# A two-layer mixture-of-experts backbone on one core: which experts share the 128 rows of a matmul unit, and the order in which their weights are loaded

## The chip, the cores and the metric

The kernel runs on one core of a Trainium2 chip. A core has a matrix engine (PE, TensorE), a vector engine (DVE), a scalar engine (ACT), a general engine (POOL, GpSimd) and a queue engine (SP) that issues most of the loads; 16 DMA engines move data between the chip's memory and the core's own buffers. The metric is the device time of one execution in microseconds (us).

## The reference

Two layers over 768 tokens (256 of context, 512 of a latent stream) of 1024 numbers each. Each layer is a mixer (projections, two attentions, a convolution, gates) and then a mixture of 32 experts. The change is in the second half, which the reference computes so:

```python
pg_top, g_sel = lax.top_k(pg, 1)                       # one of 4 groups of experts for a token
pe_top, e_sel = lax.top_k(jax.nn.softmax(le, axis=-1), TOP_K)   # two of the group's 8 experts
eid = g_sel * EXPERTS_PER_GROUP + e_sel
...
def expert_block(args):
    xe, e = args
    gu = xe @ w_gu[e]                                  # 1024 -> 512
    return (jax.nn.silu(gu[:, :D_EXPERT]) * gu[:, D_EXPERT:]) @ w_dn[e]   # 256 -> 1024
...
out = jnp.zeros_like(t).at[tok_buf].add(yb * w_buf[:, None])
```

Every token goes through two of the 32 experts, so that layer 0 has 1536 rows of work (768 tokens) and layer 1 has 1024 (only the 512 latent tokens are kept). All weights are 32-bit. An expert's weights are 3 MB, all 32 are 96 MB a layer, and every expert's weights are read once whatever the routing is.

## The kernel before

**Stages.** For each layer `mixer` runs the token mixers, `post` computes the mixer's output, the second norm and the routing, and `moe` runs the experts. In `moe` the rows of an expert's tokens are fetched by an indirect DMA (`gather`), turned by PE (`transposed`), multiplied (`up`, two halves, then `hidden` and `hidden_t`, then `down`) and written to the tokens' places in memory by another indirect DMA (`scatter`). A gather or scatter row with no token is skipped.

**Positions.** The program is fixed before the routing is known, so it is written for positions 0 to 31. Positions 0 to 4 are the five experts in `FIRST` (0, 8, 16, 24, 1), whose numbers are known beforehand. The other 27 experts stand in the order of their numbers of tokens, most first; `perm` holds that order, and `eid` the expert of each position.

**Units.** `moe` works in units of 128 rows. Before, `UNITS` says how many units hold one expert (128 rows of room), two (64 rows each) and four (32 rows each): 12, 6 and 2 in layer 0 and 8, 6 and 3 in layer 1, 20 and 17 units in all. Early positions are in the units of one. The five experts of `FIRST` come first, each alone in a unit; the others are spread evenly over the rest, and the last unit holds one expert. In a unit of two or four, `sides` cuts the 128 rows, and each matmul works on 64 or 32 rows with the weights of its expert.

**Loads.** An expert's weights come in three thirds of 1 MB: `up`'s first half, its second half, and `down`. `thirds` lists all 96 in the order in which the units use them: for each unit the first halves of its experts, their second halves, then the `down` thirds of the unit before. There are 16 slots (`slots_w`) of 1 MB in both layers. `load` puts third number k of the list in slot k mod 16, so that a load waits in SP's queue until the third 16 places ahead of it has been used; `consumed` asks for as many new loads as thirds have just been used. The first slots (`rx`) come free in `post`; the last four (`late`) exist only at its end. The first 14 thirds are of `FIRST` and are loaded before the routing is known; from the 15th on, SP must read `eid`.

**Order.** PE runs, for each unit: `up` of the first half, the turning of the unit before's hidden rows, the turning of the next unit's rows, `up` of the second half, `down` of the unit before. The rows of the last two units of a layer aren't scattered but are added by PE from `ends` at the end.

**Overflow.** If an expert has more tokens than its position has room for, `cni` is above zero and a slow general path runs (`tc.If(more > 0)`).

Of the kernel before, what the change touches and what calls it, by code (L numbers as in the profile page):

```python
# [8 lines left out]
F32 = mybir.dt.float32  # L9
# [5 lines left out]
ALU = mybir.AluOpType  # L15
AX = mybir.AxisListType
# [4 lines left out]
P = 128  # L21
# [5 lines left out]
NE = 32  # L27
# [5 lines left out]
FIRST = (0, 8, 16, 24, 1)  # L33

UNITS = ((12, 6, 2), (8, 6, 3))
RG = (3, 3)
RX = (4, 6)


@with_exitstack  # L40
def backbone(ctx: ExitStack, tc: tile.TileContext, x, c, ctx_in, c_ctx, w_ada, b_ada, w_in, sgu_gain, w_sgu,
# [1127 lines left out]
    def post(l, sl, sr, mixed, ms_done, res_src):  # L1169

        mh, ml, wA, y32, later = mixed
# [10 lines left out]
        slots_w = rx[3:] + rx[:3] + later + [lambda j=j: state["late"].tile([P, 2048], F32, name=f"late{j}_{l}")  # L1182
                                             for j in range(4)]
        state = {}


        n1, n2, n4 = UNITS[l]
        firsts = (0, n1, n1 + 2 * n2, NE)
        groups = [[tuple(range(p_, p_ + g)) for p_ in range(firsts[j], firsts[j + 1], g)] for j, g in enumerate((1, 2, 4))]

        units = groups[0][:len(FIRST)]
        last = groups[0].pop()
        del groups[0][:len(FIRST)]
        units += [u for _, _, u in sorted(((j + 0.5) / len(g_), len(g_[0]), u) for g_ in groups for j, u in enumerate(g_))]
        units.append(last)
        nu = len(units)

        def column(u):

            j = (1, 2, 4).index(len(u))  # L1200
            return sum(UNITS[l][:j]) + (u[0] - firsts[j]) // len(u)

# [6 lines left out]
        thirds += [(p_, 2) for p_ in units[-1]]  # L1209

        def load(p_, i, gu, dn):
# [54 lines left out]
        modulation("shift", 3)  # L1266
        rest = list(thirds)
        eid = pp.tile([1, NE], I32, name=f"eid{l}")
# [66 lines left out]
        def route(a):  # L1335
# [79 lines left out]
            T.matmul(pe[:, NE:2 * NE], ec[:, 1:2], perm, start=True, stop=True)  # L1415
            cn = rr.tile([1, 4], F32, name=f"cn{l}")
            for j in range(3):
                V.reduce_max(cn[:, j:j + 1], pe[:, NE + firsts[j]:NE + firsts[j + 1]], axis=AX.X)
                V.tensor_scalar(out=cn[:, j:j + 1], in0=cn[:, j:j + 1], scalar1=-float(P >> j), scalar2=0.0, op0=ALU.add,
                                op1=ALU.max)  # L1420
            V.reduce_sum(cn[:, 3:4], cn[:, 0:3], axis=AX.X)
            V.tensor_copy(cni, cn[:, 3:4])

        def placed(pt, ps):

            c0 = 0
            for j, g in enumerate((1, 2, 4)):
                w_ = P // g
                for h in range(g):
                    T.matmul(pt[w_ * h:w_ * h + w_, c0:c0 + UNITS[l][j]], ps[:, 0:w_], perm[:, firsts[j] + h:firsts[j + 1]:g],  # L1430
                             start=True, stop=True)
                c0 += UNITS[l][j]

# [158 lines left out]
        for i in sets:  # L1592
# [5 lines left out]
        return hs, w, st, (pp, tp, g1, raws, load, prefetch, rx, slots_w, yf, ms_done, rk, vv, vvs, ix, ig, cni, ws_, wv, lastp, units,  # L1598
                           column, placed, rank, firsts)

# [35 lines left out]
    def moe(l, sr, hs, st, nt, final=None):  # L1636
        (pp, tp, g1, raws, load, prefetch, rx, slots_w, yf, mixer_done, rk, vv, vvs, ix, ig, cni, ws_, wv, lastp, units, column,
         placed, rank, firsts) = st
        ntok = nt * P
# [105 lines left out]
        igo, iso = (pp.tile([P, 1], I32, name=f"{n_}{l}") for n_ in ("igo", "iso"))  # L1745
        wgo = pp.tile([P, 1], F32, name=f"wgo{l}")
        with tc.If(more > 0):
            cap = mp.tile([NE, P], F32, name="cap")
            cap2 = mp.tile([NE, P], F32, name="cap2")
            V.tensor_scalar(out=cap, in0=rank.to_broadcast([NE, P]), scalar1=firsts[1] - 0.5, scalar2=float(P // 2),  # L1750
                            op0=ALU.is_lt, op1=ALU.mult)
            V.tensor_scalar(out=cap2, in0=rank.to_broadcast([NE, P]), scalar1=firsts[2] - 0.5, scalar2=float(P // 4),
                            op0=ALU.is_lt, op1=ALU.mult)
            V.scalar_tensor_tensor(out=cap, in0=cap, scalar=float(P // 4), in1=cap2, op0=ALU.add, op1=ALU.add)
            pc = b("ax")[:, 0:NE]
# [7 lines left out]
            with tc.For_i(0, -(-(ntok - P // 4) // P), 1):  # L1763
                ino, ixo, wso = slots(mp, rko, vv, wv, nt, b)
                with tc.For_i(0, NE, 1) as e:
# [9 lines left out]
                    for i in range(2):  # L1775
                        up(pg, xT, (0,), i)
                    hT = hidden_t(hidden(pg))
                    py = b("y", D)
                    down(py, hT, (0,))
                    if l == 0:  # L1780
# [5 lines left out]
            for i in range(3):  # L1786
                load(0, i, w_gu[l, FIRST[0]], w_dn[l, FIRST[0]])

# [112 lines left out]
        for j, u in enumerate(units[-2:]):  # L1901
            scatter(None, col(ix, u) if l else ixe[:, j, 1:2], None)
        free = [s_ for s_ in range(len(slots_w)) if s_ >= RX[l]]
        yt, pts = {}, {}
# [220 lines left out]
```

## Time and profile before

| | |
|---|---|
| median of 3 runs | 1917.14 us (1915.33 to 1920.27) |
| the profiled execution's own time | 1918.57 us |
| its span, first to last instruction | 1916.8 us |
| mean granted TensorE clock, as a share of 2.4 GHz | 0.967 |
| PE busy | 1770.0 us (92%) |
| DVE, ACT and POOL busy | 1054.8, 616.1 and 218.1 us |
| read from and written to memory | 375.37 and 32.56 MB |
| mean rate over the span | 213 GB/s |

The shares are means over stages with different limits: the mixers do much arithmetic on few bytes, the experts the reverse. The experts of layer 0 run from about 786 to 1066 us, those of layer 1 from about 1629 us to the end.

### The profile page before, as it was taken

Reading aid. Unit: us, or ns where it says so; the run is one execution under the profiler, and the core shown is the slowest. Engines: PE = TensorE matmul, PEld = TensorE weight load, DVE = VectorE, ACT = ScalarE, POOL = GpSimd, SP = SyncE. Lnnn points to the kernel's source line nnn. Section 1 sums busy time; section 2 is a strip of 40 time slices with the busy share of each in tenths; the row PEclk is TensorE's granted clock in tenths of the full one; section 3 lists DMA queues with packets and bytes.
Section 4 is the critical chain, followed back from the end, with each engine's and each line's share of the span. In section 5 each row is a group of like instructions: output and inputs, shape, how many; then the busy total and the mean of one; then the engine's idle time right before and its main releaser. Section 6 shows DMA issues by size and latency. Waiting matters only on the chain. (4 is left out here: it accounts for less than half of the span.)

```text
span 1916.8 us, 25339 instructions
## 1 busy us (share of the span) xinstructions
PE 1770.0 (92%) x9530; PEld 1281.6 (67%) x9530; DVE 1054.8 (55%) x1921; ACT 616.1 (32%) x1212; POOL 218.1 (11%) x286
## 2 busy tenths in 40 slices
PE   5999999999999999699989699999999995998887
PEld 2888788888888898344433287788888895543322
DVE  3337888778778847444423456887344546221115
ACT  4425677222223323111100263676332432110001
POOL 2000121000000113211100100121000013111000
PEclk8999999999999999799999799999999997999989
DMA  8321003645567574799998824003323268699996
GB/s 299 88 85 53 1 2 98 203 162 171 164 205 249 191 267 192 277 320 402 419 417 337 224 79 128 9 1 127 110 83 110 67 236 314 236 373 421 420 421 194
DMA packets 144757, 390.80 MB, mean 204 GB/s; under 512 B 19844, under 2 KB 91892, under 8 KB 119028
## 3 DMA queue, kind: packets, MB, share of 16 engines
q1 hardware_dynamic: 128468, 356.48, 50.7%
q0 software_dynamic: 16160, 32.63, 5.5%
q8 instruction: 77, 1.26, 0.3%
q14 instruction: 52, 0.43, 0.1%
HBM read 375.37 MB, written 32.56 MB: 213 GB/s over the span
## 5 line engine op out<-in xcount | busy, mean ns | idle before, releaser
L58 PE MATMUL ps_pj<-hnh,wl 128*128 128x512 f32 (+1 forms) x1232 | 436.5, 356 | 15.6 <-ACT hnh L58 9.9
L58 PE MATMUL ps_pj<-hnl,wh 128*128 128x512 f32 (+1 forms) x1232 | 431.3, 350 | 0.9 <-DVE hnl L58 0.8
L58 PE MATMUL ps_pj<-hnh,wh 128*128 128x512 f32 (+1 forms) x1232 | 430.6, 350 | 0.0
L58 PEld LDWEIGHTS ps_pj<-hnh,wl 128*128 128x128 f32 x1232 | 233.3, 190 | 56.5 <-ACT hnh L58 14.2
L58 PEld LDWEIGHTS ps_pj<-hnl,wh 128*128 128x128 f32 x1232 | 233.9, 190 | 33.0 <-DVE hnl L58 1.9
L58 PEld LDWEIGHTS ps_pj<-hnh,wh 128*128 128x128 f32 x1232 | 233.9, 190 | 30.9 <-issue 0.2
L58 ACT ACTIVATE th<-ps_pj,vecT 128x256 f32<-128x256 f32 (+1 forms) x96 | 59.4, 619 | 353.9 <-PE ps_pj L58 311.0
L58 DVE SCALAR_TENSOR_TENSOR acc<-raw_ada,sT,acc 128x1024 f32<-128x1024 f32 x112 | 139.1, 1278 | 7.2 <-DMA raw_ada<-in_w_ada_dram 6.8
L58 PE MATMUL ps_gu<-rx,xT 128*64 128x512 f32 (+2 forms) x368 | 127.6, 643 | 7.5 <-DMA rx<-in_w_expert_gate_up_dram 7.4
L58 DVE COPY xT<-ps_tr 128x512 f32<-128x512 f32 x37 | 25.6, 691 | 162.0 <-PE ps_gu L58 99.6
L58 DVE SCALAR_TENSOR_TENSOR th<-th,ps_pb 128x256 f32<-128x256 f32 (+1 forms) x72 | 42.9, 596 | 124.7 <-PE ps_pb L58 88.7
L58 ACT ACTIVATE h<-ps_gu 128x256 f32<-128x256 f32 x37 | 14.2, 384 | 271.1 <-PE ps_gu L58 271.1
L58 DVE SCALAR_TENSOR_TENSOR yo<-ps_y,ws,g 128x1024 f32<-128x1024 f32 x33 | 42.3, 1283 | 101.4 <-PE ps_y L58 99.2
L58 PEld LDWEIGHTS ps_gu<-rx,xT 128*64 128x64 f32 (+2 forms) x368 | 40.0, 153 | 70.9 <-issue 55.2
L58 PE MATMUL ps_gu<-raw_m,xT 128*64 128x512 f32 (+2 forms) x176 | 81.2, 620 | 1.4 <-DMA raw_m<-in_w_expert_gate_up_dram 1.4
L58 PE MATMUL ps_gu<-late,xT 128*128 128x512 f32 (+2 forms) x192 | 76.1, 679 | 6.0 <-DMA late<-in_w_expert_gate_up_dram 6.0
L58 DVE TENSOR_TENSOR wl<-raw_g,wh 128x1024 fp32r<-128x1024 f32 x64 | 78.1, 1220 | 2.9 <-ACT wh L58 2.6
L58 DVE TENSOR_TENSOR pl<-ps_tr,ph 128x512 fp32r<-128x512 f32 x104 | 69.8, 686 | 13.0 <-ACT ph L58 12.0
L58 POOL DMA_INDIRECT y_d<-yo,ix x35 | 35.0, 1001 | 355.1 <-DVE yo L58 354.6
L58 PE MATMUL ps_gu<-raw_l,xT 128*128 128x512 f32 (+2 forms) x144 | 69.6, 625 | 5.4 <-DMA raw_l<-in_w_expert_gate_up_dram 5.4
L58 ACT ACTIVATE hT<-ps_h 128x256 f32<-128x256 f32 x37 | 14.2, 385 | 185.7 <-PE ps_h L58 185.7
L58 DVE TENSOR_REDUCE mx<-ps_sc 128x1 f32<-128x768 f32 (+1 forms) x80 | 67.0, 843 | 5.7 <-PE ps_sc L58 5.2
(481 smaller groups left out, 3564.4 us busy)
## 6 DMA issues: line engine op xcount, KB each, us to landing
raw_ada<-in_w_ada_dram SPq DMA_DIRECT2D x48, 1024.0 KB
rx<-in_w_expert_gate_up_dram SPq DMA_DIRECT2D x46, 1024.0 KB
raw_g<-in_w_gate_dram SPq DMA_DIRECT2D x32, 1024.0 KB
late<-in_w_expert_gate_up_dram SPq DMA_DIRECT2D x24, 1024.0 KB
late<-in_w_expert_down_dram SPq DMA_DIRECT2D x24, 1024.0 KB
raw_m<-in_w_expert_gate_up_dram SPq DMA_DIRECT2D x22, 1024.0 KB
raw_l<-in_w_expert_gate_up_dram SPq DMA_DIRECT2D x18, 1024.0 KB
raw_a<-in_w_expert_gate_up_dram SPq DMA_DIRECT2D x18, 1024.0 KB
```

Of the source, the lines that this page charges most:

```text
L58: ins = f(*a, **k)
```

## The change

The rows of a unit are cut in quarters of 32. `PLACES` gives each position a number of quarters, and `UNITS` lists, unit by unit, which sizes share it: "4" is one expert with 128 rows, "31" one with 96 and one with 32, "211" one with 64 and two with 32, "22" two with 64. Layer 0 has 18 units and layer 1 has 16. Positions 0 to 3, which hold four of `FIRST`, have 96 rows and share their units with experts of 32 rows; position 4 comes first, alone. In "31" and "211" units every matmul works on 32 rows, so an expert with 96 rows takes three matmuls for one block of weights.

The 15 thirds of `FIRST` are now all loaded before the others, and a later third takes the slot of the third whose use frees it (`place`). The order among the first 15 is by which slots are used up first over the stage. `placed` and the overflow count are rewritten for the new sizes, and the general path takes its rooms from `caps`.

```diff
-UNITS = ((12, 6, 2), (8, 6, 3))
+PLACES = ((4, 4, 12, 8), (3, 3, 9, 13))
+UNITS = ("4 31 31 31 31 22 4 22 31 22 31 4 22 31 22 31 22 4", "4 31 31 31 31 211 22 31 4 211 22 31 211 22 31 4")
...
-        units = groups[0][:len(FIRST)]
-        last = groups[0].pop()
-        del groups[0][:len(FIRST)]
-        units += [u for _, _, u in sorted(((j + 0.5) / len(g_), len(g_[0]), u) for g_ in groups for j, u in enumerate(g_))]
-        units.append(last)
+        quarters = _quarters(l)
+        of = {q: [p_ for p_ in range(NE) if quarters[p_] == q] for q in range(1, 5)}
+        kinds = [(k_, UNITS[l].split().count(k_)) for k_ in ("4", "31", "211", "22")]
+        tables = {}
+        for k_, n_ in kinds:
+            tables[k_] = []
+            for q in map(int, k_):
+                tables[k_].append((q, of[q][:n_]))
+                del of[q][:n_]
...
+            w_ = {"4": P, "22": P // 2}.get(k_, P // 4)
+            sl_, o_ = [], 0
+            for (q, _), p_ in zip(tables[k_], u):
+                sl_ += [(p_, slice(o_ + w_ * h, o_ + w_ * h + w_)) for h in range(32 * q // w_)]
+                o_ += 32 * q
+            parts_[u] = (sl_, k_)
...
+        loads_ = [x_ for x_ in thirds if x_[0] < len(FIRST)] + [x_ for x_ in thirds if x_[0] >= len(FIRST)]
+        place = {}
+        for k_, x_ in enumerate(loads_):
+            place[x_] = k_ if k_ < ns_ else place[thirds[k_ - ns_]]
+        ends_ = {place[x_]: n_ for n_, x_ in enumerate(thirds)}
+        n_first = 3 * len(FIRST)
+        early_ = sorted(range(n_first), key=lambda s_: ends_[s_])[:len(rx)]
+        turn_ = early_ + [s_ for s_ in range(ns_) if s_ not in early_]
+        slot_of = {x_: turn_.index(s_) for x_, s_ in place.items()}
+        loads_[:n_first] = [loads_[s_] for s_ in turn_[:n_first]]
...
-            s_ = thirds.index((p_, i)) % len(slots_w)
+            s_ = slot_of[p_, i]
...
-            cn = rr.tile([1, 4], F32, name=f"cn{l}")
-            for j in range(3):
-                V.reduce_max(cn[:, j:j + 1], pe[:, NE + firsts[j]:NE + firsts[j + 1]], axis=AX.X)
...
+            cn = rr.tile([1, NE + 1], F32, name=f"cn{l}")
+            V.tensor_tensor(out=cn[:, 0:NE], in0=pe[:, NE:2 * NE], in1=caps[l][0:1, :], op=ALU.subtract)
+            V.reduce_max(cn[:, NE:], cn[:, 0:NE], axis=AX.X)
+            V.tensor_scalar(out=cni, in0=cn[:, NE:], scalar1=0.0, scalar2=None, op0=ALU.max)
...
-            w_ = P // len(u)
-            return [(p_, slice(w_ * h, w_ * h + w_)) for h, p_ in enumerate(u)]
+            return parts_[u][0]
...
+def _quarters(l):
+    n = PLACES[l]
+    nf = len(FIRST) - 1
+    return [3] * nf + [4] * n[0] + [3] * n[1] + [2] * n[2] + [1] * n[3]
```

The rows below show how the instructions stand now. `ps_gu` is the result of `up`, `ps_y` of `down`; `rx`, `raw_l`, `raw_m`, `raw_a` and `late` are slots with a third of weights; `xT` and `hT` are turned rows.

PE in layer 1 before the change, the second unit (position 1 alone): its `up`, `down` of the first unit, and the third unit's `up`.

```order
L58 MATMUL ps_gu_14881<-rx5_1_13658,xT_14856 128x512 x4
L58 MATMUL ps_h_14887<-mats_60,h_14877 128x128 x2
L58 MATMUL ps_tr_14893<-mats_60,xg2_1_14598 128x128 x4
L58 MATMUL ps_tr_14899<-mats_60,xg2_1_14598 128x128 x4
L58 MATMUL ps_gu_14881<-rx0_1_13653,xT_14856 128x512 x4
L58 MATMUL ps_y_14927<-rx1_1_13654,hT_14890 128x512 x4
L58 MATMUL ps_gu_14948<-rx2_1_13655,xT_14892 128x512 x4
```

The same place after the change (positions 0 and 19):

```order
L62 MATMUL ps_gu_14995<-raw_l_14300,xT_14960 32x512 x3
L62 MATMUL ps_gu_14995<-late3_1_14649,xT_14960 32x512
...
L62 MATMUL ps_h_15014<-mats_60,h_14991 128x128 x2
L62 MATMUL ps_tr_15020<-mats_60,xg2_1_14700 128x128 x4
...
L62 MATMUL ps_gu_14995<-raw_a_14378,xT_14960 32x512 x3
L62 MATMUL ps_gu_14995<-rx3_1_13772,xT_14960 32x512
...
L62 MATMUL ps_y_15067<-rx5_1_13774,hT_15017 128x512 x4
```

The second unit now reads four thirds in its two `up` halves where it read two, and its second `up` half reads a third (in `rx3`) that is loaded only after the first unit has used that slot.

SP's queue at the end of `post` in layer 1 before the change, the last of the first 16 loads; `eid1` is the table that the routing writes.

```order
L1219 DMA late0_1_14521<-in_w_expert_gate_up_dram 128x2048
L1219 DMA late1_1_14523<-in_w_expert_down_dram 128x2048
L1279 TENSOR_LOAD eid1_13691
...
L1219 DMA late2_1_14535<-in_w_expert_gate_up_dram 128x2048
...
L1219 DMA late3_1_14547<-in_w_expert_gate_up_dram 128x2048
```

The same place after the change:

```order
L1255 DMA late0_1_14633<-in_w_expert_gate_up_dram 128x2048
L1255 DMA late1_1_14635<-in_w_expert_down_dram 128x2048
L1255 DMA late2_1_14637<-in_w_expert_down_dram 128x2048
L1315 TENSOR_LOAD eid1_13807
...
L1255 DMA late3_1_14649<-in_w_expert_gate_up_dram 128x2048
```

One load more (the 15th, in `late2`) stands ahead of the wait for the routing.

PE at the end of layer 1 before the change: `down` of the last unit but two (four experts), then `up` of the last unit, `down` of the last but one, and the last unit's second half.

```order
L58 MATMUL ps_y_16015<-raw_m_14388,hT_15987 32x512
L58 MATMUL ps_gu_16043<-raw_l_14390,xT_15989 128x512 x4
L58 MATMUL ps_y_16053<-late0_1_14521,hT_16051 64x512
L58 MATMUL ps_y_16053<-late1_1_14523,hT_16051 64x512
...
L58 MATMUL ps_gu_16043<-late2_1_14535,xT_15989 128x512 x2
```

After the change (the last unit but two holds two experts, the last but one 96 and 32 rows):

```order
L62 MATMUL ps_y_16301<-raw_m_14504,hT_16266 64x512
L62 MATMUL ps_gu_16321<-late3_1_14649,xT_16268 128x512 x4
L62 MATMUL ps_y_16331<-raw_l_14506,hT_16329 32x512 x3
L62 MATMUL ps_y_16331<-raw_a_14378,hT_16329 32x512
...
L62 MATMUL ps_gu_16321<-late0_1_14633,xT_16268 128x512 x2
```

The order of the steps is the same, and so is the number of thirds that the last unit and the one before it read in them.

## Rows read from the trace of the kernel before

**Rows 1.** The page: busy us by engine; GB/s moved in 40 slices

```profile
PE 1770.0 (92%) x9530; PEld 1281.6 (67%) x9530; DVE 1054.8 (55%) x1921; ACT 616.1 (32%) x1212; POOL 218.1 (11%) x286
...
GB/s 299 88 85 53 1 2 98 203 162 171 164 205 249 191 267 192 277 320 402 419 417 337 224 79 128 9 1 127 110 83 110 67 236 314 236 373 421 420 421 194
```

**Rows 2.** Stretches of both expert stages; last columns: clock, DMA share, GB/s

```profile
806.00:866.00 60.00, 60.00 (x192) 29.82 (x192) 26.45 (x31) 7.75 (x17) 10.12 (x10) 1.00 0.91 318
866.00:900.00 34.00, 34.00 (x148) 13.48 (x144) 15.06 (x18) 3.09 (x7) 5.07 (x5) 1.00 1.01 404
900.00:1030.00 130.00, 120.96 (x512) 46.78 (x508) 44.17 (x53) 12.62 (x29) 16.10 (x16) 0.97 1.02 419
...
1648.00:1704.00 56.00, 56.00 (x191) 26.50 (x193) 13.94 (x20) 6.77 (x15) 9.11 (x9) 1.00 0.90 319
1704.00:1752.00 48.00, 48.00 (x251) 18.52 (x243) 11.06 (x17) 5.42 (x12) 8.09 (x8) 1.00 1.02 419
1752.00:1840.00 88.00, 73.88 (x308) 24.76 (x308) 11.96 (x18) 5.95 (x14) 7.94 (x8) 0.94 1.02 421
1840.00:1862.00 22.00, 18.56 (x77) 5.25 (x78) 2.73 (x4) 1.24 (x3) 0.98 (x1) 0.84 1.01 419
...
1870.00:1874.00 4.00, 4.00 (x24) 0.96 (x17) 0.00 (x0) 0.00 (x0) 0.00 (x0) 0.57 0.74 309
...
1878.00:1882.00 4.00, 4.00 (x18) 1.06 (x16) 0.00 (x0) 0.00 (x0) 0.00 (x0) 1.00 0.27 105
```

**Rows 3.** The chain of work that ended last, layer 1: start us, us, what

```profile
1659.77 0.98 PE ps_tr L58 x8
...
1664.19 3.43 PE ps_y L58 x8
1667.62 3.43 PE ps_gu L58 x8
...
1671.28 0.96 PE ps_tr L58 x8
...
1702.83 3.57 PE ps_gu L58 x32
...
1714.96 3.63 PE ps_gu L58 x8
```

**Rows 4.** DMA queues from 1752 to 1840 us: packets, MB, share of 16 engines

```profile
q1 hardware_dynamic: 4763, 34.70, 94.6%
q0 software_dynamic: 1155, 2.33, 6.9%
```

**Rows 5.** SP's queue, layer 1: start us, us, issued loads, count

```profile
1636.34 8.63 SPq L1219 DMA_DIRECT2D rx<-in_w_expert_gate_up_dram  x2
1648.08 0.34 SPq L1219 DMA_DIRECT2D rx<-in_w_expert_down_dram  x1
...
1861.30 0.33 SPq L1219 DMA_DIRECT2D late<-in_w_expert_down_dram  x1
```

**Rows 6.** PE in order of time, ends of both stages; in brackets its waits

```profile
1036.61 3.65 PE L58 MATMUL ps_gu<-raw_a,xT 128*64 128x512 f32 x14 [1.33 <-DMA raw_a<-in_w_expert_gate_up_dram]
...
1051.66 3.70 PE L58 MATMUL ps_gu<-late,xT 128*128 128x512 f32 x8
...
1869.84 0.69 PE L58 MATMUL ps_y<-raw_m,hT 128*32 128x512 f32 x1 [1.42 <-DMA raw_m<-in_w_expert_down_dram]
...
1878.72 3.65 PE L58 MATMUL ps_y<-late,hT 128*64 128x512 f32 x16
1882.30 1.98 PE L58 MATMUL ps_gu<-late,xT 128*128 128x512 f32 x4
```

**Rows 7.** PE in order of time, the start of layer 1's experts

```profile
1628.78 1.95 PE L58 MATMUL ps_tr<-mats,y 128*128 128x128 f32 x8 [9.94 <-DMA y<-hn_d,ig]
```

**Rows 8.** Tile hn_d from 1560 to 1640 us: issue to landing

```profile
DMA to landing us min/median/max: 3.2/8.2/9.6
```

**Rows 9.** DVE in order of time, one row of the overflow count

```profile
1619.13 0.15 DVE L58 TENSOR_REDUCE cn<-ps_r 1x1 f32<-1x12 f32 x1
```

More of the change, by code (lines that the diff above doesn't have):

```diff
@@ L126, in backbone @@
     keyb, keyc, eidc = mats[0:NE, 656:688], mats[0:NE, 688:689], mats[0:NE, 689:690]
+    caps = [mats[0:NE, 700 + NE * l:700 + NE * l + NE] for l in range(2)]
     ones1 = cst.tile([P, P], F32, name="ones1")
@@ L1266, in post @@
         modulation("shift", 3)
-        rest = list(thirds)
+        rest = list(loads_)
         eid = pp.tile([1, NE], I32, name=f"eid{l}")
@@ L1415, in route @@
             T.matmul(pe[:, NE:2 * NE], ec[:, 1:2], perm, start=True, stop=True)
-            cn = rr.tile([1, 4], F32, name=f"cn{l}")
-            for j in range(3):
-                V.reduce_max(cn[:, j:j + 1], pe[:, NE + firsts[j]:NE + firsts[j + 1]], axis=AX.X)
[L1419 to L1422, printed above, removed]
-        def placed(pt, ps):
[L1426 to L1432, printed above, removed]
+            cn = rr.tile([1, NE + 1], F32, name=f"cn{l}")
+            V.tensor_tensor(out=cn[:, 0:NE], in0=pe[:, NE:2 * NE], in1=caps[l][0:1, :], op=ALU.subtract)
+            V.reduce_max(cn[:, NE:], cn[:, 0:NE], axis=AX.X)
+            V.tensor_scalar(out=cni, in0=cn[:, NE:], scalar1=0.0, scalar2=None, op0=ALU.max)
+        def placed(pt, ps):
+            for k_, n in kinds:
+                c0, o_ = first_col[k_], 0
+                for q, ps_ in tables[k_]:
+                    for p_ in ps_:
+                        if p_ == ps_[0] or p_ - 1 not in ps_:
+                            n_ = 1
+                            while p_ + n_ in ps_:
+                                n_ += 1
+                            cs = c0 + ps_.index(p_)
+                            T.matmul(pt[o_:o_ + 32 * q, cs:cs + n_], ps[:, 0:32 * q], perm[:, p_:p_ + n_], start=True,
+                                     stop=True)
+                    o_ += 32 * q
         def softmax_exp(src, mx, n, nm):
@@ L1598, in post @@
         return hs, w, st, (pp, tp, g1, raws, load, prefetch, rx, slots_w, yf, ms_done, rk, vv, vvs, ix, ig, cni, ws_, wv, lastp, units,
-                           column, placed, rank, firsts)
+                           column, placed, perm, parts_, free_)
     def spread(wv, vv, w, nt):
@@ L1746, in moe @@
         wgo = pp.tile([P, 1], F32, name=f"wgo{l}")
+        p0 = units[0][0]
         with tc.If(more > 0):
             cap = mp.tile([NE, P], F32, name="cap")
[L1749 to L1754, printed above, removed]
+            capp = mp.tile([NE, NE + 1], F32, name="capp")
+            V.tensor_tensor(out=capp[:, 0:NE], in0=perm, in1=caps[l], op=ALU.mult)
+            V.reduce_sum(capp[:, NE:], capp[:, 0:NE], axis=AX.X)
+            V.tensor_copy(cap, capp[:, NE:].to_broadcast([NE, P]))
             pc = b("ax")[:, 0:NE]
@@ L1775, in moe @@
                     for i in range(2):
-                        up(pg, xT, (0,), i)
+                        up(pg, xT, units[0], i)
                     hT = hidden_t(hidden(pg))
                     py = b("y", D)
-                    down(py, hT, (0,))
+                    down(py, hT, units[0])
                     if l == 0:
@@ L1786, in moe @@
             for i in range(3):
-                load(0, i, w_gu[l, FIRST[0]], w_dn[l, FIRST[0]])
+                load(p0, i, w_gu[l, FIRST[p0]], w_dn[l, FIRST[p0]])
         def place_weights():
@@ L1902, in moe @@
             scatter(None, col(ix, u) if l else ixe[:, j, 1:2], None)
-        free = [s_ for s_ in range(len(slots_w)) if s_ >= RX[l]]
+        free = list(free_)
         yt, pts = {}, {}
@@ L2073, in _constants @@
     m[:, 656:688], m[0:NE, 688], m[0:NE, 689] = key[None, :], key, np.arange(NE)
+    for l in range(2):
+        m[:, 700 + NE * l:700 + NE * l + NE] = 32 * np.array(_quarters(l))[None, :]
     def table(rot):
```

28 lines of the change are left out of this document (17 added, 11 removed).

## The prediction

> **What bounds the kernel now.** I read the page first: PE is busy 92% of the span and every other engine far less, but the rate of the DMA engines runs from 1 to over 420 GB/s [rows 1]. The two hills of 420 GB/s are the expert stages, and only there does the change act, so the next view is these stages cut into stretches [rows 2]. Each has two phases. At first (806 to 866 us in layer 0, 1648 to 1704 us in layer 1) PE is busy all the time at the full clock, 60.00 of 60.00 and 56.00 of 56.00 us, while the DMA engines move 318 and 319 GB/s. Later they move 419 to 421 GB/s, the highest steady rate, and PE has idle time: 73.88 of 88.00 us busy from 1752 to 1840 us. So a stage is bound by PE first and by the loads afterwards.
>
> The chain shows why. A unit with one expert takes PE from 1659.77 to 1671.28 us, 11.5 us; a unit with four takes from 1702.83 to 1714.96 us, 12.1 us [rows 3]. The price hardly depends on how many experts share a unit. The DMA price does. From 1752 to 1840 us the load queue brought 34.70 MB beside 2.33 MB of gathers and scatters [rows 4]; a third is 1.049 MB, so 33 thirds in 88 us, 2.66 us each with everything around them. One expert asks for 3 x 2.66 = 8.0 us of DMA per 11.5 us of PE: DMA idles. Four ask for 32 us per 12.1: PE idles. The five or more single units at the head of each layer waste DMA time that the quads miss later.
>
> That the low early rate is asked for and not suffered is seen in SP's queue: the 17th to 19th loads go out at 1636.34, some 8 us later, and 1648.08 us [rows 5], each when PE has used a third.
>
> **What the change does, part by part.** *Units.* After the first unit ("4"), four units of two experts each follow in both layers, then mostly pairs. Six thirds ask for 6 x 2.66 = 16.0 us of DMA per PE unit of about 12 (priced as the unit of four, the nearest row that works in 32-row pieces). Up to the third unit of layer 1 the slots come free as before, since the first unit still holds one expert: the third in hand at 1648 us is the same. From there two slots come free at almost every step of 3.4 us (`up` or `down`, [rows 3]) and two thirds cost 5.3 us, so the queue in front of the DMA engines grows, and the rate should be 420 GB/s from the third unit on.
>
> What that is worth is the bytes not moved early, at the full rate. Layer 1: (421 - 319) x 56 / 421 = 13.6 us. Layer 0: (421 - 318) x 60 / 421 = 14.7 us, and (421 - 404) x 34 / 421 = 1.4 us [rows 2]. Together 29.7 us, the most that this can give, since the same 96 thirds and the same token rows are still moved.
>
> Three things are taken off or left open.
> - *The ramp.* With one or two loads outstanding the engines will not reach 421 at once. If one unit of 12 us still runs at the old rate, that is 12 x 102/421 = 2.9 us a layer. Bounds are nothing and two units, 0 to 11.6 us in all; I take 5.8, since the queue grows by about 4 us of work a unit.
> - *Uneven engines.* At the end the rate falls from 309 (1870 us) to 105 GB/s (1878 us) [rows 2]: some of the 16 engines finish about 8 us ahead of the last. The last, which decides, is some 3.5% slower over the 234 us from 1648, so it had less idle time early: 3.5% of 56 or 60 us, 2 us a layer. Bounds 0 and 8 us in all; I take 4.
> - *The last steps.* Before, PE's last wait for a load ends at 1869.84 us for the 91st third, and the last unit's second half starts at 1882.30 us, 12.5 us later, which is five thirds at 2.49 us (1.049 MB at 421 GB/s). In layer 0 it is 1036.61 and 1051.66 us, 15 us for six [rows 6]. So the end of the loads and the last `up` coincide. After the change the last `down` but one needs the 94th third, two places before the end, and takes 3.6 us (the `ps_y` row at 1878.72 us [rows 6]): the last `up` then starts 5.0 - 3.6 = 1.4 us before the last third lands. At half clock (0.57 at 1870 us [rows 2]) it takes near 7 and starts 2 us after. I take 0, with 2 us either way per layer.
>
> *Loads.* The 15th third no longer waits for the routing. 1 MB more, 2.5 us, stands in front of the normed rows `hn_d`, whose write takes up to 9.6 us to land [rows 8], and on which the first gather of layer 1 waits (PE idle 9.94 us [rows 7]). But the same megabyte is then missing beside that gather. I take 0, with 2.5 us either way a layer. The second unit's second `up` half needs a third loaded only after 1636.34 us; it is used after the third load's issue at 1648.08 us, over 10 us later [rows 5], and the longest landing seen, 9.6 us, fits. If it came late, PE would wait there, but the end hangs on the loads, which no longer wait for PE.
>
> *Small parts.* Matmuls on 32 rows: 12.1 against 11.5 us a unit, some 0.6 us in each of four early units, on PE, which has 4 us to spare per unit as soon as the loads bind; without that cover, 5 us in both layers. `placed` goes from 7 matmuls to 6 in layer 0 and to 8 in layer 1. The overflow count goes from eight short DVE steps (0.15 us [rows 9]) to three, while PE waits for the first gather [rows 7]: nothing. The overflow path stays shut: with the reference's inputs the fullest position by this table has 30 tokens in 32 rows in layer 0 and 27 in 32 in layer 1. Gathers, scatters and their bytes are unchanged; two and one units fewer save PE some 12 us each, while PE waits for loads: nothing.
>
> **The sum.** 29.7 - 5.8 - 4 = 19.9 us. The profiled execution took 1918.57 us with 1.8 us around its span: 1898.7 us. It was 1.4 us above the median of the runs shown, so against the median 1917.14 - 19.9 = 1897 us.
>
> **Rivals.**
> *The engines were nearly full already.* The share column says 0.90 and 0.91 in the early stretches against 1.02 later [rows 2]. If that is the room there is, it is (1.02 - 0.90) x 56 / 1.02 + (1.02 - 0.91) x 60 / 1.02 + 0.3 = 13.4 us, with half the ramp and the 4 us off about 6.5: 1910.5 us. For it: the column. Against it: the same engines move 421 at 1.02, so at 0.90 they should move 371, and they move 319; a packet that waits alone counts as busy. The Trainium skill has a rule that points the same way (DMA: Bandwidth & Descriptors, "Where 436 GB/s comes from"): loads from memory are bound at about 358 GB/s per core. By that page alone the room would be (358 - 319) x 56 / 358 + (358 - 318) x 60 / 358, an estimate of 12.8 us; this trace, with 421 GB/s of loads for 88 us, differs, and the sum goes by the trace.
>
> *No net change.* The start slips by 2.5 us in each layer, the ramp takes two units, the last engine gains least, and the last steps run at half clock: 29.7 - 11.6 - 8 - 5 - 4 = 1 us, 1916 us. Each is possible, all at once hardly.
>
> *Slower: PE's clock.* Where the loads bind, PE works 12 us in 16, 75%, and in pieces. The granted clock was 0.94 with PE busy 84% from 1752 us, 0.84 from 1840 us, and 0.57 for 4 us after waits near 1870 us [rows 2]. If the mean clock falls below 12/16 = 0.75, PE becomes the bound again: at 0.65 a unit takes 18.5 us, 2.5 us above its loads, and over some nine such units in each layer that is 45 us: 1897 + 45 = 1942 us. Against it: a slower PE waits less, and the clock came back to 1.00 after each dip in these rows. The Trainium skill (TensorE: Matmul & The Clock Gate, "HAM oscillation") tells of a kernel that lost its clock at every wait for a load; here the row at 1870 us agrees with a dip, and the row from 1752 us, at 0.94, with no lasting one.
>
> **How the numbers follow.** The forecast, a gain of 10 to 30 us (1887 to 1907), has a chance of 0.75. The nearly full engines have 0.13, no change 0.05, the clock 0.07. The low end is the most that the bytes can give with the last steps as well, 1917 - 29.7 - 2 = 1886; the high end takes in most of the second case, 1910. About 0.3%, 5.8 us (1911.4), is what a measurement here tells from no change. Faster has the forecast's 0.75 and, of the nearly full engines, 0.08; same 0.05 + 0.05; slower 0.07.
>
> **What would show it.** Right: in each layer the rate passes 400 GB/s about two units after the stage's start instead of five to seven; in layer 1 PE begins to wait for loads some 40 us earlier after the stage's start than before, where it was still busy 48.00 of 48.00 us up to 1752 us [rows 2]; layer 1's stage begins 10 to 13 us earlier, and its last `up` some 20 us earlier than 1882.30 us. Wrong: an early rate that stays near 340 with a share of 1.0 (the first rival), a clock below 0.75 over the second half of a stage (the last), or a first gather that lands 2 us later. A PE that waits in the second to fifth unit would show that the shared units starve, which costs nothing unless the DMA engines idle meanwhile.

## The result, and the profile after

The changed kernel takes 1891.81 us (median of 4 runs, 1889.62 to 1893.32), the kernel before 1917.79 us in the same comparison: a ratio of 0.9866 (0.9849 to 0.9883), 26 us less. A second comparison, on another chip, gave 0.9865 (0.9845 to 0.9885). The forecast was 1897 us; the gain is 6 us larger than the 20 us foreseen.

The page of the kernel after, the lines that answer to [rows 1]: busy us by engine and the rate in 40 slices.

```profile
span 1891.5 us, 26769 instructions
...
PE 1739.8 (92%) x10296; PEld 1256.8 (66%) x10296; DVE 1042.1 (55%) x1895; ACT 611.2 (32%) x1203; POOL 210.5 (11%) x280
...
GB/s 304 90 76 64 1 2 72 209 171 170 170 196 209 265 249 171 273 367 419 418 417 355 226 79 126 15 1 129 88 107 84 94 186 340 254 419 421 418 418 196
```

PE's share is the same 92%, and it tells nothing here: the hills of 420 GB/s begin earlier in each expert stage, and this is seen only when a stage is cut up. Stretches of the kernel before that were not shown yet, from the turning of the first gathered rows to the second half of the last `up`, whole and at both ends (us, busy us and instructions of PE, PEld, DVE, ACT and POOL, granted clock, DMA share, GB/s):

```profile
786.10:806.00 19.90, 19.90 (x77) 10.55 (x78) 5.12 (x16) 1.99 (x5) 5.43 (x6) 0.86 0.59 207
786.10:1051.66 265.56, 254.16 (x988) 107.45 (x988) 99.06 (x124) 26.22 (x60) 38.67 (x39) 0.98 0.93 368
1030.00:1051.66 21.66, 19.30 (x69) 6.83 (x66) 8.25 (x8) 0.77 (x2) 1.95 (x2) 1.00 0.69 286
1628.78:1648.00 19.22, 19.22 (x72) 10.23 (x73) 3.74 (x10) 1.99 (x5) 4.01 (x4) 0.84 0.35 131
1860.00:1882.30 22.30, 18.93 (x70) 5.16 (x66) 2.13 (x3) 0.77 (x2) 0.98 (x1) 0.92 0.72 297
1628.78:1882.30 253.52, 232.59 (x950) 89.80 (x950) 45.56 (x70) 22.14 (x51) 31.11 (x31) 0.95 0.91 365
```

The same stretches of the kernel after:

```profile
789.13:815.00 25.87, 25.87 (x142) 12.57 (x142) 5.81 (x17) 2.96 (x7) 4.04 (x4) 0.89 0.56 188
815.00:870.00 55.00, 55.00 (x412) 20.19 (x409) 24.96 (x29) 5.80 (x13) 8.10 (x8) 1.00 1.01 414
...
1020.00:1039.31 19.31, 16.70 (x76) 5.12 (x72) 4.55 (x5) 0.77 (x2) 1.75 (x2) 1.00 0.69 282
789.13:1039.31 250.18, 233.78 (x1350) 88.00 (x1350) 88.15 (x112) 23.27 (x54) 32.16 (x32) 0.99 0.94 383
1615.61:1640.00 24.39, 24.39 (x140) 12.10 (x140) 4.44 (x11) 2.96 (x7) 6.83 (x7) 0.89 0.51 175
1640.00:1690.00 50.00, 50.00 (x424) 18.30 (x424) 12.13 (x18) 5.80 (x13) 8.10 (x8) 1.00 1.01 416
1690.00:1840.00 150.00, 127.62 (x712) 42.27 (x704) 23.88 (x34) 10.94 (x26) 15.02 (x15) 0.94 1.01 419
1840.00:1857.06 17.06, 16.05 (x84) 5.58 (x84) 2.13 (x3) 0.77 (x2) 0.97 (x1) 1.00 0.64 265
1615.61:1857.06 241.45, 218.06 (x1352) 78.24 (x1352) 42.58 (x66) 20.46 (x48) 30.92 (x31) 0.95 0.94 383
```

Read them as engine time lost against 421 GB/s. In layer 1, before, the first 19.22 us lost 19.22 x (421 - 131)/421 = 13.2 us and the next 56 us, at 319 GB/s [rows 2], 13.6 us; after, the first 24.39 us lose 14.3 and the next 50 us 0.6. That is 26.8 against 14.9: 11.9 us, and the stage is 12.1 us shorter. The ends, at 297 and 265 GB/s, lost 6.6 and 6.3. In layer 0 the stage is 15.4 us shorter, but it also moves less, 95.86 MB against 97.61 before, and the 1.75 MB loaded ahead of it are worth 4.2 us at 421 GB/s. Where PE waits for loads in layer 1 the clock was 0.94 (1690 to 1840 us); before it was 0.94 and then 0.84 [rows 2].

SP's queue after, layer 1 (start, us, issued loads, count), against [rows 5]:

```profile
1622.91 0.36 SPq L1255 DMA_DIRECT2D rx<-in_w_expert_gate_up_dram  x1
1631.89 0.33 SPq L1255 DMA_DIRECT2D raw_m<-in_w_expert_gate_up_dram  x1
1635.48 0.33 SPq L1255 DMA_DIRECT2D raw_l<-in_w_expert_gate_up_dram  x1
1636.06 0.33 SPq L1255 DMA_DIRECT2D late<-in_w_expert_down_dram  x1
1640.46 0.33 SPq L1255 DMA_DIRECT2D raw_a<-in_w_expert_gate_up_dram  x1
1641.05 0.33 SPq L1255 DMA_DIRECT2D rx<-in_w_expert_gate_up_dram  x1
```

From 1635 us on, 20 us into the stage, two slots come free at almost every step. The chain of work that ended last (start, us, what), against [rows 3]:

```profile
1660.87 3.57 PE ps_gu L62 x32
1664.44 3.48 PE ps_y L62 x32
1667.92 16.77 DMA rx<-in_w_expert_gate_up_dram
1684.81 24.92 DMA raw_l<-in_w_expert_gate_up_dram
1709.84 23.82 DMA rx<-in_w_expert_down_dram
```

Where the chain of before went through PE from unit to unit, it now passes to the loads at 1667.92 us, 52 us into the stage. PE in order of time, layer 1 (in brackets its waits), against [rows 6, 7]:

```profile
1615.61 1.95 PE L62 MATMUL ps_tr<-mats,y 128*128 128x128 f32 x8 [6.96 <-DMA hn_d<-hn]
...
1709.77 0.62 PE L62 MATMUL ps_gu<-raw_l,xT 128*32 128x512 f32 x1 [1.25 <-DMA raw_l<-in_w_expert_gate_up_dram]
...
1846.13 0.64 PE L62 MATMUL ps_y<-raw_m,hT 128*64 128x512 f32 x1 [0.42 <-DMA raw_m<-in_w_expert_down_dram]
...
1857.06 1.98 PE L62 MATMUL ps_gu<-late,xT 128*128 128x512 f32 x4
```

Before, the first wait for a load in this stage was:

```profile
1757.97 0.62 PE L58 MATMUL ps_gu<-rx,xT 128*32 128x512 f32 x1 [0.90 <-DMA rx<-in_w_expert_gate_up_dram]
```

So PE first waits for a load 94 us into the stage, where it was 129 us before. Not all went well: layer 0's first gathered rows are turned at 789.13 us, 3.0 us later than before, though the order of the experts, `perm`, was known at nearly the same time.

### The profile page after: what moved, and what is told of

Read it like the earlier page. It is cut to its first block, busy times and chain, and to the rows that moved or that the text cites. A ratio compares the mean times of both kernels' runs of the same rounds, so it can differ in the third digit from the quotient of the medians.

```text
span 1891.5 us, 26769 instructions
## 1 busy us (share of the span) xinstructions
PE 1739.8 (92%) x10296; PEld 1256.8 (66%) x10296; DVE 1042.1 (55%) x1895; ACT 611.2 (32%) x1203; POOL 210.5 (11%) x280
## 5 line engine op out<-in xcount | busy, mean ns | idle before, releaser
L62 PE MATMUL ps_gu<-late,xT 128*32 128x512 f32 (+2 forms) x296 | 109.4, 622 | 9.5 <-DMA late<-in_w_expert_gate_up_dram 9.5
L62 PE MATMUL ps_gu<-rx,xT 128*32 128x512 f32 (+2 forms) x448 | 101.5, 618 | 8.0 <-DMA rx<-in_w_expert_gate_up_dram 8.0
L62 PE MATMUL ps_gu<-raw_m,xT 128*32 128x512 f32 (+2 forms) x272 | 95.7, 635 | 9.1 <-DMA raw_m<-in_w_expert_gate_up_dram 9.0
L62 DVE SCALAR_TENSOR_TENSOR yo<-ps_y,ws,g 128x1024 f32<-128x1024 f32 x30 | 38.5, 1284 | 106.6 <-PE ps_y L62 106.6
L62 PE MATMUL ps_gu<-raw_l,xT 128*32 128x512 f32 (+2 forms) x328 | 90.6, 613 | 1.3 <-DMA raw_l<-in_w_expert_gate_up_dram 1.3
L62 DVE TENSOR_TENSOR pl<-ps_tr,ph 128x512 fp32r<-128x512 f32 x104 | 69.8, 687 | 12.9 <-ACT ph L62 11.9
L62 ACT ACTIVATE pr<-ps_sc,mx 128x768 f32<-128x768 f32 (+1 forms) x80 | 65.8, 824 | 13.2 <-DVE mx L62 12.4
L62 ACT CAST wh<-raw_g 128x1024 fp32r<-128x1024 f32 x64 | 66.7, 1042 | 6.6 <-DMA raw_g<-in_w_gate_dram 6.6
L62 PE MATMUL ps_pb<-ycl,bh 128*128 128x256 f32 (+1 forms) x192 | 68.3, 356 | 0.0
```

The costliest lines, as they stand in the source:

```text
L62: ins = f(*a, **k)
```

## The experiments

Each kernel was compared with the kernel before on the same chip. The table beside the medians is from one profiled execution each: the time from `perm` to the first turning of gathered rows in layer 0 (start 0) and layer 1 (start 1), and from there to the last `up` (stage 0 to its second half, stage 1 to the second block of it), all in us.

| kernel | median | ratio to before (95%) | start 0 | stage 0 | start 1 | stage 1 |
|---|---|---|---|---|---|---|
| before | 1917.79 | 1 | 7.71 | 265.56 | 12.93 | 257.25 |
| after | 1891.81 | 0.9866 (0.9849 to 0.9883) | 10.46 | 250.18 | 11.02 | 245.17 |
| after, again | 1894.26 | 0.9865 (0.9845 to 0.9885) | 12.13 | 250.24 | 10.80 | 244.80 |
| old shares, new code | 1923.66 | 1.0026 (1.0016 to 1.0035) | 11.53 | 264.26 | 11.11 | 257.29 |
| the same, 15th load late | 1920.81 | 1.0015 (1.0002 to 1.0029) | 8.02 | 265.03 | 11.20 | 256.83 |
| new shares in layer 1 only | 1914.13 | 0.9964 (0.9950 to 0.9977) | 12.53 | 265.03 | 11.16 | 245.10 |
| first five alone | 1917.59 | 0.9987 (0.9976 to 0.9997) | 12.42 | 261.49 | 11.28 | 254.53 |
| one unit more a layer | 1901.49 | 0.9907 (0.9892 to 0.9922) | 10.83 | 252.48 | 12.11 | 249.64 |
| 15th load late | 1888.00 | 0.9842 (0.9825 to 0.9859) | 8.57 | 249.90 | 10.89 | 244.54 |
| 13th to 15th late | 1895.06 | 0.9870 (0.9848 to 0.9893) | 8.59 | 252.73 | 12.36 | 244.14 |
| first pair | 1888.85 | 0.9838 (0.9816 to 0.9859) | 11.18 | 246.98 | 12.55 | 240.70 |
| first pair, 15th late | 1887.33 | 0.9830 (0.9813 to 0.9847) | 7.89 | 247.60 | 13.06 | 241.32 |
| first pair, 13th to 15th late | 1893.63 | 0.9874 (0.9857 to 0.9891) | 7.86 | 251.01 | 13.48 | 242.03 |

The time of one kernel moves by some 5 us either way between executions (the kernel before: 1914.09 to 1924.92 in 21 runs). Much of that lies outside the stages: from the last `up` of layer 0 to layer 1's `perm` the profiled executions take 558.8 to 566.0 us, while the two of the changed kernel agree within 0.4 us in both stages. So a step of the kernel is read from the columns and the sum from the ratios. Start 0 is not so steady: 10.46 and 12.13 us in these two.

**Old shares, new code.** In this and the following kernels `HEADS` gives the quarters of the first five positions, `PLACES` counts the other 27, and "1111" is a unit of four.

```diff
+HEADS = ((4, 4, 4, 4, 4), (4, 4, 4, 4, 4))
-PLACES = ((4, 4, 12, 8), (3, 3, 9, 13))
+PLACES = ((7, 0, 12, 8), (3, 0, 12, 12))
-UNITS = ("4 31 31 31 31 22 4 22 31 22 31 4 22 31 22 31 22 4", "4 31 31 31 31 211 22 31 4 211 22 31 211 22 31 4")
+UNITS = ("4 4 4 4 4 4 22 4 22 1111 4 22 4 22 4 22 1111 4 22 4", "4 4 4 4 4 22 1111 4 22 22 1111 22 4 22 1111 22 4")
```

> The new code with the old shares: the first five positions with 128 rows each and the 20 and 17 units of before, so that only the new order of the first 15 loads and the rewritten small parts are left of the change. Theory (the gain is bytes that the early shared units pull forward): nothing of the gain is left, 1917 us, within 3 of the kernel before, and the early rate in layer 1 is back near 319 GB/s. Rival 1 (the gain comes from the 15th load ahead of the routing and the new order of the slots): 1892 to 1905 us.

Measured: 1.0026, 5 us slower than before. The whole gain is gone and a cost appears; rival 1 falls. Both stages are as long as before, within 1.3 us. Its early stretches, to be compared with 318 and 319 GB/s in [rows 2]:

```profile
811.00:871.00 60.00, 60.00 (x192) 29.42 (x193) 26.91 (x31) 7.52 (x17) 11.15 (x11) 1.00 0.91 315
...
1651.00:1707.00 56.00, 56.00 (x194) 26.43 (x196) 14.06 (x20) 6.78 (x15) 9.11 (x9) 1.00 0.90 321
```

So the shares alone are worth 1.0026 - 0.9866 = 0.016 of the time, some 31 us, and the code around them costs some 5 us.

**New shares in layer 1 only.** The first halves of `HEADS`, `PLACES` and `UNITS` as in the last kernel, the second halves as in the changed one.

> The old shares in layer 0, the new ones in layer 1. Theory: layer 1 keeps what its own rows say, 12 us of its stage and some 2 us at its start, so 1904 us (1900 to 1907), and layer 0's stage is as before. Rival 2 (the gain is in the number of units, 20 to 18 and 17 to 16, at some 8.7 us for each of the three): layer 1 keeps one third, 1909 us.

Measured: 0.9964, 1914 us, above what either expected. As a ratio the rival's 1909 us is 0.9954, inside the interval (0.9950 to 0.9977), so the time alone doesn't exclude it. Against the old shares in the same code it is 0.0062, 12 us, and the rows place them: stage 1 is 245.10 us, as in the changed kernel, stage 0 265.03 us, as before. The expectation had left out the 5 us that the new code costs. In the profiled execution the first `ps_po` of layer 0, ahead of anything edited, also came 3.8 us later than with the old shares (679.7 against 675.9 us). Rival 2's one third of the gain doesn't fit the rows: layer 1 loses one unit of the three, and its stage gets 12 of the 26 us by which both stages are shorter than with the old shares.

**First five alone.** The new sizes, but the sharing of the first five positions taken away; their small partners share one unit.

```diff
+HEADS = ((4, 4, 4, 4, 4), (4, 4, 4, 4, 4))
-PLACES = ((4, 4, 12, 8), (3, 3, 9, 13))
+PLACES = ((3, 4, 12, 8), (2, 3, 9, 13))
-UNITS = ("4 31 31 31 31 22 4 22 31 22 31 4 22 31 22 31 22 4", "4 31 31 31 31 211 22 31 4 211 22 31 211 22 31 4")
+UNITS = ("4 4 4 4 4 22 4 22 31 22 31 1111 4 22 31 22 31 22 4", "4 4 4 4 4 211 22 31 4 211 22 31 1111 211 22 31 4")
```

> The new sizes, but the first five experts alone in units of 128 rows, and their four small partners together in one unit of four in the middle; 19 and 17 units. Theory: the five single units bring the low early rate back, 319 GB/s up to the fifth unit, and with it nearly the whole loss, 1914 us (1909 to 1919). Rival 2 (number of units): one unit fewer than before, 1909 us. Rival 1 (order of loads, small parts): as the changed kernel, 1892 us.

Measured: 0.9987, 1917.6 us. The low rate is back:

```profile
814.00:874.00 60.00, 60.00 (x198) 29.23 (x197) 26.22 (x30) 7.23 (x17) 9.36 (x10) 1.00 0.94 332
...
1648.00:1704.00 56.00, 56.00 (x217) 26.26 (x218) 14.11 (x20) 6.78 (x15) 9.12 (x9) 1.00 0.90 325
```

Of the 26.2 us by which the stages of the changed kernel are shorter than with the old shares (264.26 - 250.18 and 257.29 - 245.17), 5.5 us are left, which come with the other sizes. The 20.7 us lost are not all the early sharing: this kernel also has one unit more in each layer, 19 and 17. The next experiment has these numbers of units too, with the early units shared, and its stages are 9.0 and 4.9 us shorter (252.48 and 249.64 us). So 13.9 us are early sharing with the number of units held, and 6.8 us go with the two units.

**One unit more a layer**, with the early units as changed.

```diff
+HEADS = ((3, 3, 3, 3, 4), (3, 3, 3, 3, 4))
-PLACES = ((4, 4, 12, 8), (3, 3, 9, 13))
+PLACES = ((5, 4, 10, 8), (4, 3, 7, 13))
-UNITS = ("4 31 31 31 31 22 4 22 31 22 31 4 22 31 22 31 22 4", "4 31 31 31 31 211 22 31 4 211 22 31 211 22 31 4")
+UNITS = ("4 31 31 31 31 22 4 22 31 22 31 4 22 31 4 4 31 22 4", "4 31 31 31 31 211 22 31 4 211 22 31 211 4 4 31 4")
```

> The changed kernel with one pair in the later part of each layer split into two units of one expert: 19 and 17 units, the same early units. Theory: PE has 16 us of idle time in layer 0's stage and 23 us in layer 1's, so a unit of some 12 us hides in each: 1892 to 1897 us, most of any loss in layer 0, where only some 4 us of idle time would be left. Rival 2 (number of units, by PE's time): two units of 12 us come back, 1916 us; by the 128 skipped rows of a gather and a scatter alone: 1896 us.

Measured: 0.9907, some 8 us slower than the changed kernel (0.9907 - 0.9866), between the theory's 0 to 5 and the rival's 24, nearer to the rival's second form (1896 us). By the rows the stages are 2.3 and 4.5 us longer. In the changed kernel PE was busy 15.35 of 20.00 us from 1000 us on and 16.05 of 17.06 us from 1840 us on; here it has hardly any idle time left near the end of either stage (the last row is of layer 1):

```profile
870.00:1000.00 130.00, 123.23 (x614) 46.40 (x613) 46.77 (x55) 11.51 (x27) 17.84 (x18) 0.99 1.01 417
1000.00:1020.00 20.00, 20.00 (x100) 7.57 (x98) 7.82 (x11) 2.10 (x5) 1.23 (x2) 1.00 1.01 414
1020.00:1040.30 20.30, 19.41 (x90) 6.26 (x89) 7.02 (x8) 1.15 (x3) 1.95 (x2) 1.00 0.61 248
...
1836.00:1857.20 21.20, 21.20 (x122) 7.17 (x120) 3.42 (x5) 1.15 (x3) 1.94 (x2) 1.00 0.55 229
```

In layer 0 PE is busy 244.82 of the stage's 252.48 us: most of a unit hides in PE's waits, but not all, and with the 20 units of before PE alone would need some 12 us more than this (an estimate), longer than the stage after (250.18 us). Why the larger loss is in layer 1, where the theory had expected the smaller, is not shown beyond that busy end. Rival 2 falls as the main cause: with the 17 units of before, layer 1 keeps 7.6 of its 12.1 us (249.64 against 257.25 and 245.17). But the units saved are not nothing either.

**15th load late.** The changed kernel with one load put back behind the wait for the routing.

```diff
-                    if p_ < len(FIRST):
+                    if p_ < len(FIRST) and len(rest) != len(loads_) - 3 * len(FIRST):
```

> The changed kernel, with the 15th load (the last third of the fifth expert) issued after the wait for the routing, as before the change. Theory: in layer 0 the first gather lands some 2 us earlier after the routing, and the same megabyte is then missing later, where the loads bind, at 2.5 us a layer: no change beyond 2 us against the changed kernel. Rival 1, now for a loss (the 15th load costs the 4.5 us by which the new code with the old shares was slower than the kernel before): 4 us faster than the changed kernel.

Measured: 0.9842, 1888.0 us (1885.86 to 1890.96) against 1894.26 (1892.17 to 1896.43) for the changed kernel in the same comparison: 6 us faster, and the theory's "no change" falls; rival 1's 4 us is nearest. PE in order of time, the first gathered rows of layer 0:

```profile
785.51 1.95 PE L64 MATMUL ps_tr<-mats,y 128*128 128x128 f32 x8 [4.79 <-DMA y<-hn_d,ig]
```

They are turned 8.57 us after `perm`, where the changed kernel needs 10.46 and 12.13. Against its execution in the same comparison, starts and stages together are 4.1 us shorter, 3.6 of them at start 0; some 2 us of the 6 are not placed. The stretches of the same stage:

```profile
785.50:811.00 25.50, 25.49 (x142) 12.43 (x142) 6.43 (x18) 2.96 (x7) 5.60 (x6) 0.90 0.73 258
811.00:866.00 55.00, 55.00 (x412) 20.16 (x409) 24.90 (x29) 5.80 (x13) 8.10 (x8) 1.00 1.01 413
...
785.51:1035.41 249.90, 233.51 (x1351) 87.87 (x1351) 88.74 (x113) 23.27 (x54) 33.74 (x34) 0.99 0.96 391
```

The stage takes 249.90 us as before the edit (250.18), and moves more in it, 97.61 against 95.86 MB. The load went into the first 25 us, at 258 against 188 GB/s, where the engines had room; it is not missed. Over all kernels the two groups don't touch: 10.46 to 12.53 us in the seven with the 15th load ahead, 7.71 to 8.59 in the six with it behind, 3.5 us between their means. In layer 1 there is no such difference.

**Old shares, 15th load late.** The same edit in the kernel with the old shares.

> The new code with the old shares, and the 15th load after the wait for the routing. Theory (what the new code costs is the 15th load ahead of the first gather of layer 0): as the kernel before, within 2 us, where the new code with the old shares alone was 1.0026 of it; in layer 0 the first gather is turned some 8 us after perm, not 11.5. Rival (the new order of the slots or the rewritten small parts cost it): 1.002 to 1.003 of the kernel before again.

Measured: 1.0015 (1.0002 to 1.0029), between the two. In layer 0 the first gather is turned 8.02 us after `perm`, as the theory says, but some 3 us (1.0015) are left by the ratio, whose interval begins at 1.0002. Their place is not found: stages and starts are each as long as in the kernel before or shorter, start 0 but for 0.3 us. Part of the new code's cost stays open.

**13th to 15th late.** The same line with `len(loads_) - len(rest) < 13`.

> As the kernel with the 15th load after the routing, but with the 13th and 14th there too. Theory (in the first 25 us of a stage the DMA engines have room for five thirds, so that loads moved behind the first gather aren't missed): the first gather of each layer is turned 1 to 2 us sooner after the order of the experts (perm) is known, and the stage is no longer: 1885 us (1882 to 1888) against 1888.0 with the 15th alone. Rival 1 (it was the 15th alone that stood in front of the gather): 1888 us. Rival 3 (the thirds are missed): PE waits for a third of a known expert in the first 45 us of the stage, 1890 us or more.

Measured: 0.9870, by the ratios some 5 us slower than with the 15th alone (0.9842; the intervals overlap). The theory falls: the starts are not shorter (8.59 and 12.36 us), and stage 0 is 2.8 us longer. Rival 3's reason fails too, as PE waits for no load in the first 45 us of a stage. Stage 0 moves 99.70 MB where it moved 97.61: 2.09 MB more, 5.0 us at 421 GB/s, of which less than half was caught up. SP's queue at the start of layer 0's experts:

```profile
788.07 1.50 SPq L1257 DMA_DIRECT2D late<-in_w_expert_down_dram  x2
790.10 0.34 SPq L1257 DMA_DIRECT2D late<-in_w_expert_gate_up_dram  x1
806.16 0.35 SPq L1257 DMA_DIRECT2D rx<-in_w_expert_gate_up_dram  x1
```

The rate of the DMA engines from 784 to 812 us, in 40 slices of 0.7 us:

```profile
GB/s 0 0 0 0 129 123 351 445 375 416 398 421 427 386 375 380 345 445 392 380 410 375 398 351 334 351 281 293 240 135 64 12 0 187 187 433 456 222 12 0
```

The next load goes out at 806.16 us, 9.6 us after the first half of the first `up` had ended (4.38 us from 792.14 us; with the 15th alone, 1.1 us after 787.33 + 5.39 us), and just when the engines run dry, at 12 GB/s. SP's own instructions fill the time. After the four loads it comes to the branch of the overflow path (`tc.If`, L1787), and then it reads 13 numbers of experts from `eid` into its registers (L1317):

```profile
L1787 SPq COMPARE_BRANCH  x1: 45/45/45, 791.2 to 791.2; - x1
L1787 SPq EVENT_SEMAPHORE  x6: 17/17/17, 791.3 to 797.3; - x6
L1317 SPq TENSOR_LOAD <-eid x13: 263/271/522, 797.6 to 805.4; - x13
```

With the 15th alone the same 13 reads run from 784.7 us on and end at 793.2 us, just behind that half `up`. So the late loads put SP at the branch later (791.2 against 783.4 us), it is held there for 6 us instead of 1 (by what, the trace doesn't show), and the reads then stand ahead of the next load.

**First pair.** Two of the known experts, of few tokens, share the first unit, so that sharing begins one unit earlier.

```diff
-FIRST = (0, 8, 16, 24, 1)
+FIRST = (8, 16, 0, 24, 1)
+HEADS = ((2, 2, 3, 3, 3), (2, 2, 3, 3, 3))
-PLACES = ((4, 4, 12, 8), (3, 3, 9, 13))
+PLACES = ((4, 3, 14, 6), (3, 2, 11, 11))
-UNITS = ("4 31 31 31 31 22 4 22 31 22 31 4 22 31 22 31 22 4", "4 31 31 31 31 211 22 31 4 211 22 31 211 22 31 4")
+UNITS = ("22f 31 31 31 22 4 22 31 22 31 4 22 31 22 4 22 22 4", "22f 31 31 31 211 22 31 4 211 22 31 4 211 22 22 4")
```

> Shares from the first unit on: the first unit holds two of the five known experts with 64 rows each, the next three one known expert with 96 rows and one small one; 18 and 16 units as in the changed kernel. Theory: the first two steps free two slots instead of one each, so two thirds of 2.5 us are moved some 10 us earlier in each layer, and the time falls by 5 us a layer, to about 1882 us (1878 to 1887); the rate passes 400 GB/s one step earlier. Rival 2 (number of units): no change from the changed kernel, 1892 us. Rival 3 (the second unit starves, since its small expert's halves are asked for only by the first unit's steps): PE waits before 20 us into the stage, and the gain is lost.

Measured: 0.9838, 1888.9 us, 5 us below the changed kernel in the same comparison (1894.26); 10 were expected, and the intervals of the two ratios overlap. By the rows the mechanism holds and most of its size: the stages are 3.2 and 4.5 us shorter than those of the changed kernel (250.18 and 245.17 us). SP's queue in layer 1:

```profile
1624.07 0.36 SPq L1257 DMA_DIRECT2D rx<-in_w_expert_gate_up_dram  x1
1624.68 0.33 SPq L1257 DMA_DIRECT2D raw_m<-in_w_expert_gate_up_dram  x1
1633.36 0.33 SPq L1257 DMA_DIRECT2D raw_l<-in_w_expert_gate_up_dram  x1
1634.20 0.33 SPq L1257 DMA_DIRECT2D raw_a<-in_w_expert_down_dram  x1
```

The first two steps free two slots each. Rival 2 falls, as the number of units is that of the changed kernel, and so does rival 3: PE waits for no load in the first 20 us of either stage. Start 1 is 1.5 us longer.

**First pair with the late loads.**

> Both edits: two known experts in the first unit, and the 15th load after the wait for the routing. Theory: as the first unit with two experts alone, within 2 us, about 1882 us. Rival 1: 4 us less than that, 1878 us.

> The kernel with two known experts in the first unit, and the 13th to 15th load after the routing. Theory: as far below 1887.3 us (the same with the 15th alone) as the other run of this call is below 1888.0: 1884 us. Rival 3: the first pair uses the slots sooner, so that the thirds are missed more: 1890 us.

Measured: 0.9830 and 0.9874. The first is the lowest ratio of all, but its interval (0.9813 to 0.9847) doesn't part it from the 15th load late alone (0.9825 to 0.9859): start 0 is 3.3 us shorter than with the first pair alone, the stages are not. Either version beats the changed kernel (1894.26 us in the same comparison) by 6 to 7 us. The second falls back like the 13th to 15th late, and SP's queue shows the same there: four loads by 788.71 us, the branch, 13 reads, the next load at 803.69 us.

## Why the prediction was right

*The room was right, and nearly all of it was had.* The most that the bytes could give was put at 29.7 us. The stages became 15.4 and 12.1 us shorter, 27.5 us, of which 4.2 us are bytes that layer 0 loaded ahead of its stage; the shares alone are worth some 31 us by the ratios. The step that made it is the one named: two slots at a time from the early shared units on. With the first five alone most of it is lost, with a first pair it grows. Its signs came: over 400 GB/s from 24 to 26 us into each stage on, PE's waits 35 us earlier in layer 1, that stage's start 13.2 us earlier and its last `up` 25.2 us earlier. One sign that it had called wrong came too, a first gather 2 us later (3.0 us, in layer 0); it came with the 15th load and not with the shares.

*The ramp was too large.* 5.8 us were taken off. Layer 1 shows 13.6 - 11.9 = 1.7 us. In layer 0 of the kernel with the 15th load late, which moves the same bytes in the stage as before, the first 25.50 us lose 9.9 and the next 55 us 1.0, against 10.1, 14.7 and 1.4 before: 0.8 us of 16.1. Together 2.5 us.

*The uneven engines do not show.* 4 us were taken off because the engine that ends last would gain less. The ends lost 6.9 and 6.6 us of engine time before and 6.4 and 6.3 after. So these rows show nothing of this term.

*The last steps* were put at 0, with 2 us either way; the two ends together are 0.8 us better.

*The loads were not free.* The step "I take 0" for the 15th load failed in its reason, that the same megabyte is then missing beside the gather: with the load late the stage does not get longer, since the engines have room in its first 25 us. So the delay that it causes in front of the first gather of layer 0, 3.5 us, is a cost; it lies in layer 0, not in layer 1, of which the prediction had spoken.

*Small parts.* Of `placed` only the number of its matmuls was given, and no time was put on it. It is on the way to the first gather. PE in order of time before, layer 1:

```profile
1616.41 1.12 PE L58 MATMUL ps_tr<-perm,pixs 32*128 32x8 f32 x14
```

The same place after:

```profile
1605.15 2.23 PE L62 MATMUL ps_tr<-perm,R__14588 32*128 32x3 f32 x18
```

The 18 matmuls (nine a table, not the eight counted) take 1.1 us more than the 14 before; in layer 0 it is 0.6 us. As start 1 is shorter all the same, this cost is not seen by itself. The units saved were priced at nothing as well; one unit put back shows 2.3 us in layer 0 and 4.5 us in layer 1.

The sum, then: 27.5 us from the stages (29.7 less 2.5, the ends nearly even), 3.0 lost at layer 0's start, 1.9 won at layer 1's (12.93 to 11.02 us; the old shares in the new code show the same, and its cause was not sought), 1.1 lost between the stages: 25.3 us, as the spans say (1916.8 and 1891.5). The stages gave 7.6 us more than the 19.9 forecast, and 2.2 us that had been left out were lost around them: that the time came out nearer than the terms is luck.

*The rivals.* The engines were not nearly full: the share column rose from 0.90 to 1.01 while the rate rose from 319 to 416 GB/s. The Trainium skill (DMA: Bandwidth & Descriptors, "Where 436 GB/s comes from") would end the loads at about 358 GB/s per core; 419 GB/s over 150 us here differs. The Trainium skill's page Perfetto Trace Analysis (section "Roofline"), by which a core that is alone gets more than that share, up to about 435 GB/s, agrees. The clock rival needed a mean below 0.75; it was 0.94 from 1690 to 1840 us with PE busy 85% of the time. The Trainium skill's "HAM oscillation" (TensorE: Matmul & The Clock Gate), a clock lost at every wait for a load, is not what this trace shows; its waits for loads in layer 1, at most 2.65 us (at 1717.22 us), are shorter than those of the page's kernel.

## What to carry to other kernels

Where one stage is bound first by arithmetic and then by loads, price it by the bytes that the idle engines could have moved early, and look for the order of work that frees buffers sooner; the total of either said little here. Take nothing off that estimate without a row for it: of the 9.8 us taken off here, 2.5 showed. One load moved into the idle stretch cost nothing here, and ahead of the gather on which the stage's start hangs it cost 3.5 us; but three moved there did not all fit, so the idle stretch has to be measured first, with the instructions that the queue's own engine must run between its loads.

## What was not expected of the hardware

The DMA share says 0.90 at 319 GB/s and 1.01 at 416: with few loads in the queue it overstates how full the engines are. A unit cut into 32-row pieces keeps PE hardly longer than one of 128 rows: 3.57 us for 32 matmuls of an `up` half in the chain after, 3.43 us for 8 before [rows 3]. And reading numbers into SP's registers is slow enough to count: 13 reads of `eid` took 8.3 us (797.6 to 805.9 us, with the 13th to 15th load late), in which SP issued no load.
